# Warm-up products of a two-layer decoder: rounded, 512 columns wide, with a new order of issue

## The chip, the core and the metric

The kernel runs on one core of one Trainium2 chip. Its time is the device time of one execution in microseconds (us); of several runs the median counts. The core has five engines that work side by side: TensorE (in the profile PE for its products and PEld for the loads of stationary operands), VectorE (DVE), ScalarE (ACT), GpSimd (POOL) and SyncE (SP), which here issues most transfers. The transfers of the program and the blocks of the engines' own instructions are carried by the same 16 DMA engines.

## The reference

It computes a decoder trunk of two layers over a sequence of 256 tokens of width 1024, batch 1, in float32:

```
c_act = silu(c)
for layer in (0, 1):
    shift, scale, gate = split(c_act @ w_ada[layer] + b_ada[layer], 3)
    h = rms_norm(x, norm_g[layer]) * (1 + scale) + shift
    y = even_mixer(h) if layer == 0 else odd_mixer(h)
    x = x + gate * y
return rms_norm(x, final_g)
```

`even_mixer` projects h once, feeds a sliding-window attention with sinks and a three-branch sparse attention, multiplies each by a SiLU gate and projects the result out. `odd_mixer` does the same with a block-sparse attention, which at 256 tokens is plain causal attention within one block.

## The kernel before

The products with weights are kept accurate by splitting each operand into a rounded part and a remainder (`whi`, `wlo` of the weights, `hhi`, `hlo` of the activations). Three rounded products (type F32R) then stand for one in float32: hi by hi, hi by lo and lo by hi (`mm3`). A float32 product (type F32) that is no transpose goes through TensorE as two loads and two passes. A rounded product, and a transpose, is one load and one pass.

All operations are recorded first (`Plan.record`) and then issued in a fixed order, the list `ORDER` of their record numbers. `FLIP` lists operations that go to the other one of VectorE and ScalarE than the code names. Each engine runs its own instructions in the order of that list, so a later instruction waits behind an earlier one that is not ready.

The start of the program runs as follows. x and the small vectors are loaded. TensorE runs products of a tile of ones that nobody reads (12 into the bank of `ring_warm`, 20 into that of `keep`), so that it isn't idle ahead of its first real work. c is put through SiLU into `cz`; x is normalised and transposed into `bigA`. The columns of `w_ada` for shift and scale come in five groups (`START`). The first group covers 128 columns of shift and of scale: four transfers of 256 KB into `qT`. The second covers 256 columns of each: eight transfers of 256 KB, two each into a third `qT` tile, `gate`, `oT` and `kTb`. Of the second group, VectorE sums the rows that lie in `qT` and `gate` into `acc` (`start_sums`, d = 4), and TensorE sums those in `oT` and `kTb` directly and then adds `acc`, all in the bank `ps_m`. From a group's sums follow shift and scale (`shs`), from these `hhi` and `hlo`, and then the products of that piece of h with its rows of `w_in_even` (`start_mm`), which come through `raw` in two transfers a row (652 KB and 192 KB).

In the order before, the transfers of SP begin: x in two pieces, one of the first group, the 652 KB row piece, one of the first group, the 192 KB piece, two of the first group, then the second group as `oT`, `oT`, `qT`, `qT`, `gate`, `gate`, `kTb`, `kTb`, then the next rows of `w_in_even`. VectorE adds the `gate` rows to `acc` right after those of `qT`, then forms `hlo` of the first piece and, when TensorE has the sums of the second group, copies them out (`asb`). TensorE does 13 rounded products of the first piece ahead of the sums over `kTb` and `acc`.

Of the kernel before, what the change touches and what calls it, by code (L numbers as in the profile page):

```python
# [13 lines left out]
P = 128  # L14
# [21 lines left out]
49 7 6 4 0 1 9 21 22 23 2 3 47 5 91 41 42 48 92 89 24 25 26 27 28 29 30 93 73 88 50 31 90 32 74 99 58 33 75 34  # L36
98 35 51 77 59 94 52 76 36 46 44 45 60 54 37 53 10 11 38 61 12 13 14 63 95 78 79 15 97 16 132 17 126 96 64 128
101 127 18 19 20 62 129 100 102 103 104 105 106 107 108 109 110 111 112 113 114 115 116 117 130 133 55 83 158
118 65 56 66 68 80 67 119 159 84 85 121 86 120 81 131 69 122 174 175 176 177 178 179 180 181 168 82 70 143 160
140 170 134 123 137 87 171 39 161 40 124 149 138 169 172 155 150 146 144 71 162 135 173 72 147 141 125 163 182  # L40
183 184 185 186 187 188 189 190 191 192 193 152 194 142 195 153 201 165 196 136 197 151 199 198 164 154 156 202
148 203 157 139 200 238 207 226 204 205 239 240 166 214 227 208 228 206 220 209 167 232 215 235 212 236 241 268
221 280 242 243 269 218 223 281 233 210 145 229 230 278 216 213 237 222 244 211 250 270 234 282 259 262 271 251
283 224 252 279 225 247 219 265 284 256 272 231 245 257 285 263 273 286 287 288 289 290 291 292 293 217 294 295
296 297 264 298 258 299 307 274 246 300 248 301 249 275 303 302 260 266 253 308 254 309 255 267 261 324 304 336
311 305 310 337 333 277 345 318 325 306 346 339 313 276 338 312 342 319 314 343 372 326 316 344 315 348 373 380
322 8 381 320 378 379 375 374 377 376 472 530 334 327 328 382 335 360 366 361 383 362 329 349 340 341 350 347
369 330 384 331 332 354 385 363 351 357 317 386 387 388 389 390 391 392 393 394 395 396 397 321 355 398 356 323
399 367 405 400 368 401 364 402 358 359 406 365 370 407 371 352 403 442 409 443 408 430 436 411 473 418 410 353
433 424 527 420 445 404 431 434 412 446 413 425 421 533 427 428 416 432 439 422 474 414 423 475 1003 939 476 691  # L50
477 417 415 435 444 466 429 451 440 441 447 437 463 478 480 482 484 479 481 483 485 486 487 438 488 460 419 489
495 454 455 491 490 469 470 493 464 492 426 496 448 499 457 467 494 497 471 529 456 500 509 501 449 498 510 511
524 450 502 503 617 525 452 458 618 465 619 620 531 453 468 461 550 506 462 942 459 556 512 551 513 813 514 526
507 554 504 557 508 552 505 521 555 522 534 518 536 553 515 537 516 541 538 519 606 542 520 938 539 517 535 607
528 544 543 608 937 547 540 676 564 565 566 567 568 569 576 694 577 612 578 579 609 580 581 588 589 590 613 558
523 610 611 591 592 593 549 600 601 602 559 639 545 692 603 604 621 614 622 623 624 560 695 561 625 548 562 563
570 571 615 572 605 573 626 627 640 631 628 629 632 641 574 575 630 582 693 583 633 634 635 814 935 636 643 644
645 646 584 642 638 585 940 586 587 647 594 595 670 596 597 669 546 598 637 599 668 648 649 816 650 651 663 653
661 662 696 697 698 699 700 671 654 701 652 702 664 703 818 943 689 819 936 655 817 656 43 657 665 658 704 666
705 706 667 707 708 815 709 660 710 711 659 672 673 712 713 674 714 715 716 944 717 941 746 747 748 749 945 532  # L60
683 675 946 947 948 949 754 950 951 952 953 750 752 954 955 956 957 756 753 958 959 960 961 677 684 1029 751 678
774 775 776 777 962 1032 682 757 758 780 679 680 963 685 681 718 820 782 781 964 778 719 821 686 759 784 687 720
755 822 721 722 786 688 723 965 823 971 824 779 724 966 972 785 868 869 870 871 760 967 787 968 872 761 878 969
783 768 973 974 975 976 977 978 979 980 876 981 982 983 984 763 874 985 986 987 988 769 762 788 880 1150 879 789
970 896 897 898 899 1030 1218 989 877 764 765 881 904 990 796 825 906 725 991 873 902 726 826 791 727 728 992
729 900 730 875 731 993 732 827 616 908 766 797 994 882 998 995 1000 1001 999 1031 767 1087 1088 1089 1090 996
790 905 770 1002 771 1648 1221 997 1033 772 828 1091 829 1004 830 690 831 1005 832 883 733 1093 1006 773 734
1097 1007 901 833 1095 834 792 1092 1008 793 794 891 1113 1114 1115 1116 1151 885 795 1009 1010 1011 1012 903
1034 798 799 1013 800 835 735 909 736 836 884 837 838 801 839 1152 1037 737 738 890 739 740 907 1014 886 887
1015 888 1121 1096 840 1350 741 1016 742 1094 841 1349 1123 842 1038 843 1017 1039 889 1040 844 1117 845 1035  # L70
743 910 846 1119 847 848 849 911 1219 892 850 1122 1041 1042 1043 851 1118 1153 1154 1155 1156 919 1018 1036 744
893 852 1098 853 894 1044 1045 1019 1046 913 1339 1047 854 1220 855 912 856 1048 1049 895 1050 1051 1052 1020
1053 1054 857 1157 1222 858 1419 859 1159 914 915 916 1418 1163 802 803 804 805 806 807 808 809 1160 1021 1161
917 1022 1099 1223 918 1124 1179 1180 1181 1182 1120 1100 1023 745 1164 920 921 922 1055 1056 1102 1024 1057
1189 1058 1059 1107 1060 1025 1226 1227 923 1228 1125 1183 1061 1062 1126 1108 860 810 1063 1064 1229 1230 1026
1101 1027 1187 1162 861 1340 862 863 1127 1065 1231 864 1133 1232 1233 1234 1028 865 1235 1185 1224 1236 1237
1103 1341 1104 1105 924 925 926 927 928 929 930 931 1106 1158 1225 1426 1128 811 1276 1277 1278 1279 866 1351
1423 1109 1134 1422 1110 1111 1066 1165 1188 1238 1282 1239 1240 1241 1067 1112 1284 1068 1166 1286 1069 1174
1070 1242 1352 1243 1129 1130 1184 1131 1244 1285 1071 1245 1072 1073 1167 1074 1280 1075 1427 1246 1247 1248
1249 1250 1251 1252 1253 1254 1132 1420 1186 1190 1076 1077 812 1255 1173 1135 1136 1137 1168 1191 1421 1302  # L80
1303 1304 1305 1138 1436 1342 1343 1344 1345 1312 1428 1169 1287 1306 1170 1171 1429 1192 1256 867 1078 1172
1079 1257 1258 1080 1199 1308 1259 1260 1313 1261 1262 1263 1264 1265 1281 1266 1267 1268 1283 1269 1081 1082
1310 1437 1083 1194 1175 932 1176 1177 1084 1450 1311 1270 1346 1451 1178 1288 1452 1424 1646 1193 1271 1272
1273 1085 1453 1195 1196 1274 1197 1289 1086 1353 1354 1355 1356 1198 1200 1425 1359 1139 1140 1141 1142 1143
1144 1145 1146 1147 1148 1307 933 1309 1275 1432 1440 1433 1201 1361 1202 1203 1357 1454 1430 1204 1444 1445
1290 1446 1291 1447 1448 1363 1442 1449 1292 1149 1293 1294 1431 1205 1206 1207 1208 1209 1210 1211 1212 1213
1214 1379 1380 1381 1382 1438 1297 1314 934 1508 1296 1295 1315 1439 1317 1316 1298 1362 1299 1215 1300 1493
1455 1364 1441 1456 1492 1457 1216 1462 1347 1463 1301 1458 1385 1464 1358 1459 1217 1318 1322 1465 1319 1360
1434 1320 1460 1461 1323 1468 1469 1365 1321 1387 1470 1366 1443 1466 1367 1324 1325 1368 1326 1471 1467 1327
1474 1435 1374 1496 1472 1369 1370 1526 1497 1371 1328 1329 1330 1331 1332 1333 1334 1335 1336 1337 1389 1509  # L90
1372 1383 1527 1373 1390 1384 1375 1494 1376 1377 1386 1534 1535 1388 1558 1536 1378 1391 1475 1392 1537 1495
1393 1538 1559 1394 1560 1528 1473 1395 1400 1396 1510 1397 1399 1561 1338 1562 1511 1398 1476 1529 1348 1563
1401 1402 1403 1477 1404 1478 1498 1479 1405 1406 1407 1408 1409 1410 1411 1412 1413 1414 1499 1530 1415 1539
1649 1540 1531 1416 1650 1588 1417 1512 1513 1541 1542 1564 1565 1480 1481 1543 1486 1487 1482 1488 1483 1489
1484 1490 1485 1491 1544 1500 1532 1545 1778 1566 1546 1504 1547 1548 1533 1549 1567 1550 1655 1568 1551 1501
1552 1717 1553 1554 1505 1502 1555 1556 1656 1557 1506 1503 1514 1515 1516 1517 1582 1651 1507 1653 1583 1569
1839 1518 1584 1652 1570 1571 1572 1573 1574 1575 1576 1589 1659 1519 1590 1520 57 1521 1591 1522 1657 1577 1523
1578 1524 1592 1593 1525 1654 1594 1595 1596 1579 1598 1580 1660 1581 1597 1605 1606 1585 1599 1601 1600 1667
# [1302 lines left out]
```

## Time and profile before

| what | value |
|---|---|
| median of 3 runs | 294.72 us (294.68, 294.72 and 314.98) |
| the profiled execution | 295.43 us |
| its span, first to last instruction | 293.7 us |
| PE busy | 283.5 us |
| DVE busy | 253.0 us |
| ACT busy | 201.2 us |
| instruction blocks of the largest instruction queue | 17 packets, 0.28 MB |

The profiled execution took 1.73 us around its span, and is 0.71 us above the median of the runs. A busy PE in the profile can be a PE that runs at a slower pace, since ends of products are modelled. The idle time of an engine costs something only where another engine waits for its result.

### The profile page before, as it was taken

What the parts mean: (1) busy time and instruction counts of PE and PEld (TensorE: products, weight loads), DVE (VectorE), ACT (ScalarE), POOL (GpSimd) and SP (SyncE); (2) the same over time, 40 slices, a digit from 0 to 9 for tenths busy, and PEclk for the clock granted to TensorE, in tenths of its full rate; (3) what the DMA queues carried; (4) which work ended last, traced back from release to release, by engine and by line L of the source; (5) the groups of instructions that cost most, each with busy time, mean ns of one, the idle gap of its engine ahead of it and who ended that gap; (6) DMA issues with size and microseconds to landing.
All of it is one profiled execution on the core that took longest, in us unless ns stands there. A gap on an engine that the chain in (4) does not pass through costs nothing.

```text
span 293.7 us, 6077 instructions
## 1 busy us (share of the span) xinstructions
PE 283.5 (97%) x2244; PEld 243.5 (83%) x2244; DVE 253.0 (86%) x612; ACT 201.2 (69%) x513; POOL 5.5 (2%) x27
## 2 busy tenths in 40 slices
PE   8989999999999999999899999999999999999991
PEld 7868888997789888777667799999799899887891
DVE  0669999999999999999899868898699889889973
ACT  5554746695999999996398744466667377783821
POOL 2100000000000000000000000000000000000000
PEclk9999999999999999999999999999999999999998
DMA  7999999987996787799996449608927661604003
GB/s 260 364 385 377 383 355 353 311 287 237 342 400 212 264 281 293 213 323 361 305 372 216 146 143 329 243 4 296 351 71 249 237 234 34 227 27 145 1 15 129
DMA packets 50557, 71.76 MB, mean 244 GB/s; under 512 B 2792, under 2 KB 36192, under 8 KB 50528
## 3 DMA queue, kind: packets, MB, share of 16 engines
q1 hardware_dynamic: 50128, 70.95, 70.7%
q10 hardware_dynamic: 400, 0.43, 0.4%
q8 instruction: 17, 0.28, 0.4%
q14 instruction: 12, 0.10, 0.1%
HBM read 70.32 MB, written 1.06 MB: 243 GB/s over the span
## 4 chain that ended last, share of the span: by engine, by line
PE 73%; DVE 13%; DMA 8%; issue 2%; ACT 2%; SPq 0%; DVEq 0%
PE ps_pj L276 49%; PE ps_s L276 9%; PE ps_pt L276 6%; DVE raw L276 5%; PE ps_o L276 4%; PE ps_m L276 4%; DMA kTb<-in_w_ada_dram 3%; DMA raw<-in_w_ada_dram 2%; DVE wlo L276 2%; DMA qT<-in_w_ada_dram 2%; DMA xs<-in_x_dram 1%; DVE t L276 1%; DVE oT L276 1%; ACT t L276 1%; DVE bigA L276 1%
## 5 line engine op out<-in xcount | busy, mean ns | idle before, releaser
L276 ACT CAST whi<-raw 128x512 fp32r<-128x512 f32 (+2 forms) x108 | 71.6, 689 | 33.6 <-PE ps_pj L276 15.8
L276 DVE TENSOR_TENSOR wlo<-raw,whi 128x512 fp32r<-128x512 f32 (+2 forms) x92 | 70.8, 792 | 6.4 <-ACT whi L276 6.4
L276 PE MATMUL ps_pj<-hlo,whi 128*128 128x256 f32 x256 | 70.8, 284 | 0.0
L276 PE MATMUL ps_pj<-hhi,wlo 128*128 128x256 f32 x256 | 70.0, 284 | 0.3 <-DVE wlo L276 0.3
L276 PE MATMUL ps_pj<-hhi,whi 128*128 128x256 f32 x256 | 69.9, 284 | 0.0
L276 PEld LDWEIGHTS ps_pj<-hlo,whi 128*128 128x128 f32 x256 | 48.0, 189 | 0.6 <-issue 0.3
L276 PEld LDWEIGHTS ps_pj<-hhi,wlo 128*128 128x128 f32 x256 | 47.4, 189 | 0.7 <-DVE wlo L276 0.5
L276 PEld LDWEIGHTS ps_pj<-hhi,whi 128*128 128x128 f32 x256 | 47.4, 188 | 0.3
L276 ACT ACTIVATE sm<-sm,mn 128x256 f32<-128x256 f32 (+1 forms) x58 | 25.9, 449 | 6.9 <-DVE mn L276 6.9
L276 PE MATMUL ps_pj<-whi,hhi 128*128 128x512 f32 (+2 forms) x72 | 25.8, 368 | 0.5 <-ACT hhi L276 0.4
L276 PE MATMUL ps_pj<-whi,hlo 128*128 128x512 f32 (+2 forms) x72 | 26.1, 374 | 0.0
L276 PE MATMUL ps_pj<-wlo,hhi 128*128 128x512 f32 (+2 forms) x72 | 26.0, 370 | 0.0
L276 DVE SCALAR_TENSOR_TENSOR wlo<-raw,whi 128x512 fp32r<-128x512 f32 x32 | 20.6, 686 | 3.7 <-ACT whi L276 3.6
L276 PE MATMUL ps_pj<-wlo,ghi 128*128 128x512 f32 (+1 forms) x56 | 20.4, 368 | 0.0
L276 PE MATMUL ps_pj<-whi,ghi 128*128 128x512 f32 (+1 forms) x56 | 20.4, 369 | 0.0
L276 PE MATMUL ps_pj<-whi,glo 128*128 128x512 f32 (+1 forms) x56 | 20.0, 367 | 0.0
L276 ACT ACTIVATE sm<-sm,rc 128x256 f32<-128x256 f32 (+1 forms) x41 | 17.3, 449 | 2.3 <-DVE rc L276 2.3
L276 DVE SCALAR_TENSOR_TENSOR raw<-raw,cz,raw 128x1024 f32<-128x1024 f32 x14 | 17.9, 1276 | 1.0 <-DMA raw<-in_w_ada_dram 0.9
L276 DVE SCALAR_TENSOR_TENSOR acc<-raw,cz,acc 128x1024 f32<-128x1024 f32 x14 | 17.9, 1278 | 0.1
L276 PEld LDWEIGHTS ps_pj<-whi,hhi 128*128 128x128 f32 x72 | 13.6, 188 | 2.7 <-ACT hhi L276 1.2
L276 PEld LDWEIGHTS ps_pj<-whi,hlo 128*128 128x128 f32 x72 | 13.5, 188 | 2.5 <-DVE hlo L276 0.8
L276 PE MATMUL ps_pt<-ident,sm 128*128 128x128 f32 x87 | 15.5, 279 | 0.0
(252 smaller groups left out, 599.7 us busy)
## 6 DMA issues: line engine op xcount, KB each, us to landing
raw<-in_w_in_odd_dram SPq DMA_DIRECT2D x16, 1024.0 KB, 7.5
raw<-in_w_ada_dram SPq DMA_DIRECT2D x8, 1024.0 KB, 6.2
raw<-in_w_ada_dram SPq DMA_DIRECT2D x16, 512.0 KB, 5.2
raw<-in_w_in_even_dram SPq DMA_DIRECT2D x8, 652.0 KB, 7.2
raw<-in_w_in_even_dram SPq DMA_DIRECT2D x5, 1024.0 KB, 7.7
raw<-in_w_out_even_dram SPq DMA_DIRECT2D x4, 1024.0 KB, 5.4
raw<-in_w_out_odd_dram SPq DMA_DIRECT2D x4, 1024.0 KB, 5.0
qT<-in_w_ada_dram SPq DMA_DIRECT2D x12, 256.0 KB, 6.2
```

The costliest lines, as they stand in the source:

```text
L276: self.ops.append(dict(key=eng.key, deps=deps, fn=lambda: getattr(real, name)(*args, **kw)))
```

## The change

The tile of ones shrinks to two columns, which the table-loading activations still read. The products that nobody reads take a rounded tile of ones, 512 columns wide, that lies in the space of `ghi` (which is written for good only later in layer 0); `ghi` is therefore allocated earlier. A memset on VectorE fills those 512 columns ahead of the first product. The number of the products stays at 32. Each becomes one load and one pass of 512 columns in place of two loads and two passes of 128 columns.

`ORDER` and `FLIP` are replaced. Since one operation is added, every record number above 6 is one higher. Apart from that memset the operations are the same. At the start:

- SP: x in two pieces, one transfer of the first group, the 192 KB piece, one of the first group, the 652 KB piece, the two `qT` transfers of the second group, the last two of the first group, then `oT`, `oT`, `kTb`, `gate`, `kTb`, `gate`, then the next rows.
- ACT: c is fetched ahead of the two small matrices, and the first half of x is normalised ahead of the second.
- PE: 11 unread products, the transpose of c, 6 more, then transposes of x with the other 15 unread products in between; 12 rounded products of the first piece; the sums over `kTb` and `acc`; then the products with `hlo`.
- DVE: the two additions of `gate` rows to `acc` come after the shift and scale of the first group and the remainders `wlo` of its weights, then `hlo` of the first piece, then the copy of the sums (`asb`). Two copies of transposed x into `bigA` (128x512) move from ACT to DVE.
- Further on, `FLIP` moves 21 more operations from ACT to DVE and 19 from DVE to ACT (of those, five each way between the first projections and the end of layer 0's attention), and neighbouring instructions change places on all engines. The last 94 or so operations of PE keep their places.

```diff
-    ones = const([P, P], "ones")
+    ones = const([P, 2], "ones")
+    ghi = const([P, KT, S], "ghi", F32R)
+    ones_r = ghi[:, 0:2, :].rearrange("p a b -> p (a b)")
     ring_warm = bank("m")
+    V.memset(ones_r.bitcast(F32), 1.0)
     V.memset(ones, 1.0)
     dummy = const([P, 2], "dummy")
     A.activation(dummy[:, 0:1], ones[:, 0:1], AF.Exp)
     for _ in range(WARM):
-        T.matmul(ring_warm[:, :P], ones, ones, start=True, stop=True)
+        T.matmul(ring_warm, ones_r[:, :P], ones_r, start=True, stop=True)
     keep = bank("o")
     for _ in range(20):
-        T.matmul(keep[:, :P], ones, ones, start=True, stop=True)
+        T.matmul(keep, ones_r[:, :P], ones_r, start=True, stop=True)
...
-    ghi = const([P, KT, S], "ghi", F32R)
...
 ORDER = [int(i) for i in """
-49 7 6 4 0 1 9 21 22 23 2 3 47 5 91 41 42 48 92 89 24 25 26 27 28 29 30 93 73 88 50 31 90 32 74 99 58 33 75 34
...
+3 7 2 5 6 4 91 94 89 93 95 96 90 92 100 99 101 97 102 98 59 74 0 1 42 48 49 43 60 61 46 47 75 76 45 44 62 63 22
+23 24 25 26 27 28 29 30 31 32 51 133 52 53 54 78 129 77 131 33 34 35 36 37 38 69 70 71 72 55 64 79 80 65 10 11
...
```

## Rows read from the trace of the kernel before

**Rows 1.** Busy time of each engine by stretches of 20 us (us, instructions, clock, DMA).

```profile
core 0: us, PE busy (x) PEld busy (x) DVE busy (x) ACT busy (x) POOL busy (x), PEclk, DMA share, GB/s
0.00:20.00 20.00, 17.64 (x172) 15.56 (x173) 7.91 (x20) 10.15 (x19) 3.17 (x18) 1.00 0.95 333
20.00:40.00 20.00, 20.00 (x144) 16.94 (x143) 18.77 (x38) 10.79 (x23) 0.00 (x0) 1.00 1.07 381
40.00:60.00 20.00, 20.00 (x135) 17.60 (x130) 18.81 (x45) 14.39 (x39) 0.00 (x0) 1.00 1.00 323
60.00:80.00 20.00, 20.00 (x205) 16.72 (x204) 19.53 (x71) 15.89 (x52) 0.38 (x3) 1.00 0.90 297
...
120.00:140.00 20.00, 20.00 (x138) 14.88 (x137) 19.92 (x38) 17.44 (x44) 0.00 (x0) 1.00 0.94 329
140.00:160.00 20.00, 18.73 (x91) 13.05 (x90) 18.12 (x37) 13.95 (x33) 0.61 (x2) 1.00 0.90 304
160.00:180.00 20.00, 19.71 (x137) 18.03 (x138) 16.16 (x30) 12.05 (x24) 0.00 (x0) 1.00 0.55 174
```

**Rows 2.** The chain of waits in order of time, first 22 us (start us, us, what).

```profile
0.80 3.82 DMA xs<-in_x_dram
...
5.06 5.94 DMA qT<-in_w_ada_dram
...
11.01 7.55 DMA kTb<-in_w_ada_dram
...
18.61 0.86 PE ps_m L276 x24
19.47 0.67 PE ps_s L276 x2
...
20.25 0.23 PE ps_s L276
...
21.14 0.12 PE ps_pt L276
```

**Rows 3.** Who waited for whom, 17 to 20.2 us (us in total, times, longest).

```profile
ACT whi L276 <- DMA raw<-in_w_in_even_dram: 2.6, 1, 2.6
DVE asb L276 <- PE ps_m L276: 1.9, 1, 1.9
...
PE ps_m L276 <- DMA kTb<-in_w_ada_dram: 1.1, 1, 1.1
```

**Rows 4.** DMA traffic from 0 to 16.3 us, then queues from 16.3 to 18.6 us.

```profile
DMA packets 4988, 5.20 MB, mean 319 GB/s; under 512 B 294, under 2 KB 4583, under 8 KB 4988
...
q1 hardware_dynamic: 290, 0.88, 97.9%
q8 instruction: 1, 0.02, 3.2%
```

**Rows 5.** The page's row of that instruction queue over the whole span.

```profile
q8 instruction: 17, 0.28, 0.4%
```

**Rows 6.** Busy time and instructions from 0 to 16.3 and from 16.3 to 17.2 us.

```profile
0.00:16.30 16.30, 15.06 (x140) 13.89 (x141) 6.32 (x17) 9.56 (x18) 3.17 (x18) 1.00 0.94 319
16.30:17.20 0.90, 0.90 (x7) 0.66 (x5) 0.86 (x2) 0.38 (x1) 0.00 (x0) 1.00 1.06 413
```

**Rows 7.** Instructions in order of time, start of the span (start us, us, engine).

```profile
0.90 0.17 DVE L276 MEMSET ones<- 128x128 f32 x1 [0.90 <-PEq L1386]
...
1.71 3.84 PE L276 MATMUL ps_o<-ones 128*128 128x128 f32 x20
...
5.63 1.60 PE L276 MATMUL ps_o<-ones 128*128 128x128 f32 x12
...
14.20 0.37 PE L276 MATMUL ps_pt<-whi,hhi 128*128 128x256 f32 x1
...
14.45 0.48 DVE L276 TENSOR_SCALAR acc<-qT,cz 128x512 f32<-128x512 f32 x1
...
15.75 1.54 DVE L276 SCALAR_TENSOR_TENSOR acc<-gate,cz,acc 128x512 f32<-128x512 f32 x2
...
17.20 0.42 DVE L276 TENSOR_TENSOR hlo<-oT,hhi 128x256 fp32r<-128x256 f32 x1
```

**Rows 8.** DVE groups, shapes apart (busy us, mean ns).

```profile
L276 DVE COPY bigA<-ps_pj 128x512 f32<-128x512 f32 x4 | 2.7, 686 | 0.0
L276 DVE TENSOR_SCALAR sm<-sm,rc 128x128 f32<-128x128 f32 x9 | 2.4, 279 | 0.1
```

255 rows, old and new, of tables (FLIP, ORDER) are left out of this document.

## The prediction

> **What bounds the kernel now.** I read the busy time by stretches first [rows 1]. From 20 us on PE is full, and it has visible gaps only in 140 to 180 us (1.27 and 0.29 us). DVE is nearly as full: 57.11 of the 60 us from 20 to 80, and 19.92 of 20 in 120 to 140. So two engines share the bound from 20 to about 145 us, and PE alone holds it after 165. The reader should see that little is to be had there by moving instructions about. Only the first 20 us have room: 2.36 us on PE, 12 on DVE, 9.9 on ACT.
>
> The chain of waits says what those 20 us hang on [rows 2]: the loads of x, then of `qT`, then of `kTb`, which lands at 18.57 us. The list of waits [rows 3] shows three engines held at once: PE 1.1 us for `kTb`, DVE 1.9 us for PE's sums, ACT 2.6 us for the next rows of `w_in_even`, which travel behind `kTb`.
>
> Is that landing a matter of bandwidth? The transfers up to `kTb` sum to 1024 KB of x, 12 x 256 KB of `w_ada`, 652 + 192 KB of weights and 36 KB of small ones: 4976 KB, 5.10 MB. By 16.3 us 5.20 MB had moved [rows 4]. So the bytes were there about 2 us before the landing was told. What lies between is one packet of another queue, of instructions [rows 4]. There are 17 such packets of 16 KB, and they took 0.4% of 16 engines' 293.7 us [rows 5]: 18.8 us, or 1.1 us each. One packet occupies one of the 16 DMA engines, and a transfer that is spread over all of them has landed when the last has done its share. This is an inference: a `kTb` share queued behind the packet comes 1.1 us late.
>
> A block of 16 KB at 64 bytes holds 256 instructions. My count of the order gives 4488 loads and passes on PE, which makes 17.5 blocks and fits the 17 packets. So this is PE's own program, and it is asked for when PE has got to a certain instruction. At 16.3 us PE had started 281, at 17.2 us 293 [rows 6].
>
> **The change part by part.**
> *The unread products.* Before, 32 products are 64 loads and 64 passes; after, 32 and 32. PE's program is 64 instructions shorter, all ahead of the first projection. Time per product: 20 passes took 3.84 us and 12 took 1.60 [rows 7], so a product of two passes took 0.38, later 0.27 us. A rounded product of 512 columns steps at 0.23 us [rows 2]; early it may take up to twice that. Ahead of the second small transpose stand 17 products, 4.0 to 8.0 us. They start after a memset of 512 columns, between the 0.17 us of the 128-column one and the 0.48 us of a 512-column operation [rows 7]. I take 0.4. They end by 5.3 to 9.5 us. All this costs nothing as long as the first projection waits for loads, to 14.2 us [rows 7]; without that cover it would cost up to 2 us.
>
> *Where the block falls.* In the old order PE's count is 288 at the end of the 13 rounded products, just ahead of the `kTb` sums. In the new one the `kTb` sums begin at 224 and the `acc` sums end at 272. So 281 to 293 lies 5 to 10 products behind both. The packet then can't sit ahead of `kTb` or `gate`: those loads must have landed for PE to get there. Landing without the packet is between 16.3 (the bytes) and 17.5 us (18.57 less 1.1); I take 17.0. The next rows of weights move forward too, by up to 1.1 us of ACT's 2.6 us wait.
>
> The Trainium skill speaks against this step: "Runtime: NRT & Kernel Launch", section "Instruction fetch mechanics", has the engine fetch its next block of 256 instructions while it runs the current one, so that crossing a boundary costs little and is mostly hidden. By that the block would cost nothing, and the time would stay at 294.7. It is the first rival below.
>
> *The order of the loads.* The last two transfers of the first group now stand behind two of the second: 512 KB, about 1.4 us at the 0.38 MB per us of rows 1. The first projection moves from 14.2 to some 15.6 us. The 12 rounded products ahead of the `kTb` sums have as many columns as the 13 before (2.5 us at 0.23, 0.19 by proportion, and 0.12 for 512, 408 and 256 columns [rows 2]). They end at 18.1 us; with the sums PE is at 18.75. Before, PE waited in that time, so the delay is covered.
>
> *`gate` last.* Its rows go through DVE: 1.54 us for two additions [rows 7]. From 17.0 to 17.5 this gives 18.55 to 19.05. The four `acc` products follow, and `hlo`, which now stands behind the additions on DVE, takes 0.42 us [rows 7]: 19.0 to 19.5 us. PE needs it for its next product. Before, real products resumed at 19.47 [rows 2]. PE gains 0 to 0.5 us. Behind the additions also wait `asb` and the shift and scale of pieces 1 and 2.
>
> *DVE afterwards.* Its copy of the sums comes up to 0.5 us earlier, and with the weights there 1.1 us earlier it has `wlo` to do where it waited. So DVE gains 0.1 to 1.0 us. As DVE and PE share the bound up to 145 us, I take the middle, 0.6.
>
> *The flips and the rest.* Two copies of 0.69 us [rows 8] go to DVE inside its 12 idle us: nothing, while they lie there, and 1.4 us if they fell later. Up to the end of layer 0's attention five small operations go each way (0.28 us and up [rows 8]) and nearly cancel. What the neighbours' changes of place do after 20 us no row shows. Bounds: they can gain no more than a part of the 1.56 us of PE gaps in 140 to 180 and of the 2.89 us of DVE idle in 20 to 80 [rows 1], and may lose as much. I take zero, and 1.5 us either way for the range. The last 94 operations of PE keep their order, so the tail is the same. POOL's memsets and ACT's small loads are early and idle-covered: zero, up to 0.3 us.
>
> *Sum.* 295.43 (span 293.7 and 1.73 around it) - 0.6 = 294.8 for an execution like the profiled one, which stands 0.71 above the median of the runs. The median becomes 294.1.
>
> **The rivals.**
> *The packet was not the cause, or the gain is given back* (0.2): 294.7. For it: 16 other packets fall in the span, and PE shows no gap like that beside them; what DVE is given earlier may only wait later. Against: bytes there by 16.3, landing told at 18.57.
> *The new order also trims the gaps* (0.18): half of 1.56 and a quarter of 2.89 us, together 1.5 more: 292.6. For: these are the only stretches with room, and flips move operations there. Against: in 120 to 140 us PE and DVE are both full.
> *`gate` is caught* (0.13): slower. If the sequencer asks for the block well ahead of what PE has started, more than some 60 instructions ahead, the packet arrives before the last `gate` transfer. It then lands at 18.57 as `kTb` did, and 1.54 + 0.42 us of DVE still follow: 20.5 in place of 19.47, 1.0 to 1.1 us late on both engines: 295.8. The point that decides is whether the packet starts before `gate` has landed. Against: in the old trace the packet came with PE at 281 to 293 and waiting for `kTb` at 292, which leaves the sequencer little room to lead.
> *The wider products don't keep PE ready* (0.04): if PE stepped at half pace through the first piece, 12 products would take 5.0 in place of 2.5 us: 2.5 us more than the forecast and 0.6 of lost gain, 297.2. The granted clock reads 1.00 throughout rows 1, so nothing in the trace speaks for it.
>
> **How the numbers follow.** The forecast, 294.1, has 0.45, and its own width is 293.4 to 294.9. With rivals of 294.7, 292.6, 295.8 and 297.2 at the chances above, and 1.5 us either way for the order after 20 us, the range is 292.0 to 296.4. A change of 2%, 5.9 us, is about what a measurement of this kernel can tell from no change. It would need under 288.8 or over 300.6; no case gets there. I leave 0.02 for faster (gaps on three engines closing at once) and 0.03 for slower (half pace over more than one piece).
>
> **What would show it.** Right: 32 loads and 32 passes on ones; no wait of PE, DVE or ACT for a load of 1 us or more between 16 and 20 us; the first instruction packet after 18 us; sums over `kTb` and `acc` done and `hlo` products running by 19.0 to 19.5 us; the first `whi` of the second piece well ahead of 20.05. Then the lead of about 0.6 us should still be there at 100 us and where the last projection begins. Wrong: the packet still at 16 to 17 us, a landing of `gate` past 18, or a lead at 20 us that is gone by 145 us. The forecast fails most easily through the order of the middle, of which I know places but no waits.

## The result, and the profile after

The median rose from 294.72 to 298.71 us (297.69 to 299.17). The ratio to the kernel before is 1.0139, with a 95% interval of 1.0112 to 1.0165. So the change made the kernel slower by 1.4%, where the prediction had 0.2% faster, and the time lies above its range. It is still within the 2% that the chances called no change.

The profiled execution of after took 297.69 us (span 296.0), the shortest of its runs, while that of before, 295.43 us, was longer than four of the five runs of before in this comparison (the fifth, a slow one of 314.98 us, is left out of the ratio). So the two traces differ by 2.3 us and the medians by 4.0. Part of the loss can't be seen in this pair.

The kernel after, busy time by stretches, columns as in [rows 1]:

```profile
0.00:20.00 20.00, 18.41 (x138) 13.61 (x139) 9.31 (x23) 9.78 (x19) 3.07 (x18) 1.00 0.96 321
20.00:40.00 20.00, 19.47 (x119) 16.25 (x118) 18.27 (x38) 10.20 (x22) 0.00 (x0) 1.00 1.07 372
...
140.00:160.00 20.00, 17.48 (x82) 12.06 (x81) 16.82 (x32) 12.40 (x26) 0.63 (x3) 1.00 0.79 273
```

Against [rows 1] two things stand out. From 20 to 40 us PE, which was full, has a gap of 0.53 us, and the transfers move less (321 and 372 GB/s in place of 333 and 381). From 140 to 160 us, where layer 0 ends and the first weights of layer 1 come in, PE is idle for 2.52 us in place of 1.27.

The chain of waits of after at the start, which answers to [rows 2]:

```profile
1.79 4.83 DMA rows<-in_b_ada_dram
...
6.63 0.37 SPq L274
...
8.35 6.27 DMA oT<-in_w_ada_dram
...
14.63 8.44 DMA raw<-in_w_in_even_dram
```

`kTb` is no longer on it. But the small load of `b_ada`, which now is the last of the three on ACT's queue, holds SP until 6.63 us, and a row of `w_in_even` lands only at 23.07 us. That row is the third transfer of its kind; it stood at 22.15 us in before, and it now lies behind a transfer into `t`. PE waits for what comes of it:

```profile
24.80 0.45 PE L274 MATMUL ps_o<-wlo,hhi 128*128 128x408 f32 x1 [0.53 <-DVE wlo L274]
```

The instruction block moved as forecast. The queues of after from 18.8 to 20.2 us, which answer to [rows 4]:

```profile
q1 hardware_dynamic: 327, 0.54, 105.5%
q8 instruction: 1, 0.02, 5.1%
```

Then the layer change. PE's waits in after from 138 to 170 us (us in total, times, longest); before had one of 0.8, one of 0.4 and one of 0.3 there:

```profile
PE ps_pj L274 <- ACT t L274: 1.4, 1, 1.4
PE ps_pj L274 <- ACT hhi L274: 1.1, 1, 1.1
PE ps_pj L274 <- DVE hlo L274: 0.4, 1, 0.4
```

The 0.8 us of before is this line:

```profile
PE ps_s L276 <- DVE wlo L276: 0.8, 1, 0.8
```

It is about what that execution has above its median, and the profiles of late_sqrt, products_alone, products_padded and before_shifted, all with the old order, don't have it.

And what ACT of after did ahead of the first of after's three waits, in order of time:

```profile
146.79 1.14 ACT L274 CAST whi<-raw 128x512 fp32r<-128x512 f32 x2 [1.86 <-DMA raw<-in_w_in_odd_dram]
...
149.07 1.13 ACT L274 CAST whi<-raw 128x512 fp32r<-128x512 f32 x2
150.11 0.58 ACT L274 COPY t<-ps_m 128x512 f32<-128x512 f32 x1
150.70 1.28 ACT L274 ACT_TABLE_LOAD   x1
152.00 0.20 ACT L274 ACTIVATE parts<-parts 128x1 f32<-128x1 f32 x1
...
152.61 1.33 ACT L274 ACTIVATE t<-xs,parts 128x512 f32<-128x512 f32 x2
```

The reader should see an engine without a pause for 7 us, a table load for the square root in its middle, and both halves of the normalised tokens on it, one behind the other. In the order before, a dummy Sqrt brought this load at 139.4 us, while ACT was idle. In the new order that dummy stands behind the real Sqrt (places 1841 and 1581).

### The profile page after: what moved, and what is told of

Read it like the earlier page. It is cut to its first block, busy times and chain, and to the rows that moved or that the text cites. A ratio compares the mean times of both kernels' runs of the same rounds, so it can differ in the third digit from the quotient of the medians.

```text
span 296.0 us, 6012 instructions
## 1 busy us (share of the span) xinstructions
PE 284.9 (96%) x2212; PEld 241.4 (82%) x2212; DVE 253.1 (86%) x617; ACT 201.1 (68%) x509; POOL 5.8 (2%) x27
## 4 chain that ended last, share of the span: by engine, by line
PE 76%; DVE 10%; DMA 7%; ACT 3%; issue 2%; SPq 1%; ACTq 0%; DVEq 0%
PE ps_pj L274 51%; PE ps_s L274 10%; PE ps_pt L274 6%; PE ps_o L274 6%; PE ps_m L274 3%; DMA raw<-in_w_in_even_dram 3%; DMA oT<-in_w_ada_dram 2%; ACT t L274 2%; DMA rows<-in_b_ada_dram 2%; DVE raw L274 2%; DVE t L274 2%; DVE wlo L274 1%; DVE oT L274 1%; DVE bigA L274 1%; DVE sm L274 1%
## 5 line engine op out<-in xcount | busy, mean ns | idle before, releaser
L274 PE MATMUL ps_pj<-hhi,whi 128*128 128x256 f32 x256 | 70.7, 286 | 0.0
L274 ACT ACTIVATE sm<-sm,mn 128x128 f32<-128x128 f32 (+1 forms) x58 | 26.1, 452 | 7.1 <-DVE mn L274 7.1
L274 PE MATMUL ps_pj<-wlo,ghi 128*128 128x512 f32 (+1 forms) x56 | 20.2, 367 | 0.0
L274 DVE TENSOR_TENSOR t<-ps_pj,tb 128x512 f32<-128x512 f32 (+2 forms) x22 | 12.0, 586 | 7.4 <-PE ps_pj L274 7.4
L274 ACT ACTIVATE whi<-raw 128x512 fp32r<-128x512 f32 x16 | 9.7, 626 | 10.4 <-PE ps_pj L274 9.3
L274 ACT ACTIVATE sm<-sm,rc 128x256 f32<-128x256 f32 (+1 forms) x36 | 15.7, 461 | 1.6 <-DVE rc L274 1.5
```

The source lines that it names most:

```text
L274: self.ops.append(dict(key=eng.key, deps=deps, fn=lambda: getattr(real, name)(*args, **kw)))
```

## The experiments

My first theory, T1: the time is lost in the layer change, by that table load and by the order of the two halves of the tokens. Its rivals, R1: it is lost in the prologue and in the loads; R2: it is a spread from run to run. All medians and ratios stand in one table; each ratio is to runs of before in the same series. A is the start of the last product of layer 0's attention in the profiled execution, B the way from there to the last product of the kernel, us:

| kernel | median | ratio to before, 95% | A | B |
|---|---|---|---|---|
| before | | 1 | 137.9 | 149.2 |
| after | 298.71 | 1.0139 (1.0112 to 1.0165) | 138.4 | 151.3 |
| sqrt_ahead | 298.03 | 1.0135 (1.0106 to 1.0164) | 140.1 | 151.5 |
| late_sqrt | 295.59 | 1.0039 (1.0024 to 1.0054) | 137.8 | 148.7 |
| sqrt_behind_ghi | 298.40 | 1.0138 (1.0121 to 1.0155) | 139.0 | 151.8 |
| products_alone | 295.41 | 1.0037 (1.0022 to 1.0051) | 138.6 | 148.0 |
| order_alone | 298.39 | 1.0142 (1.0120 to 1.0164) | 138.8 | 151.5 |
| products_padded | 294.38 | 1.0004 (0.9991 to 1.0017) | 137.8 | 148.2 |
| before_shifted | 295.36 | 1.0038 (1.0025 to 1.0050) | 139.1 | 148.4 |
| after_padded | 298.25 | 1.0129 (1.0108 to 1.0150) | 138.8 | 153.5 |
| new_to_140 | 297.34 | 1.0082 (1.0054 to 1.0111) | 138.9 | 150.7 |
| old_to_140 | 297.40 | 1.0106 (1.0081 to 1.0131) | 138.2 | 151.0 |
| new_to_60 | 297.66 | 1.0121 (1.0101 to 1.0141) | 140.2 | 148.6 |
| old_new | 296.06 | 1.0057 (1.0038 to 1.0077) | 137.4 | 149.4 |
| new_old | 296.38 | 1.0071 (1.0046 to 1.0096) | 138.7 | 149.0 |
| halves_back | 300.10 | 1.0192 (1.0173 to 1.0210) | 138.7 | 153.3 |
| old_new_order | 299.48 | 1.0172 (1.0149 to 1.0196) | 137.5 | 154.6 |
| old_flips | 294.66 | 1.0017 (1.0001 to 1.0034) | 137.4 | 148.5 |
| new_old_loads | 302.48 | 1.0282 (1.0262 to 1.0302) | 141.2 | 153.0 |
| after_loads | 304.93 | 1.0350 (1.0323 to 1.0377) | 141.9 | 155.0 |

**The table load.** Three kernels move the dummy Sqrt and nothing else.

```diff
 sqrt_ahead, ORDER of after (1589 is the dummy Sqrt, 1590 the real one, 1417 the cast of oT to ghi)
-1651 1416 9 1417 1532 1418
+1651 1416 9 1589 1417 1532 1418
 late_sqrt, ORDER of before (1588 the dummy, 1589 the real one)
-1531 1416 1650 1588 1417 ... 1575 1576 1589 1659
+1531 1416 1650 1417 ... 1575 1576 1589 1588 1659
 sqrt_behind_ghi, ORDER of after
-1416 9 1417 1532 1418
+1416 9 1417 1589 1532 1418
```

sqrt_ahead: 

> The changed kernel with one operation of its order moved: the dummy Sqrt that loads ScalarE's table in the layer change goes from behind the real Sqrt to right behind the dummy Exp, about 139 us, where ScalarE has idle time. T1 (the loss is in the layer change, and the 1.28 us table load at 150.7 us is on its chain): 0.7 to 1.5 us faster than the changed kernel, so about 297.4 us and a ratio of 1.009; the table load is seen near 139 us and not after the sum of squares. R1 (the loss comes from the prologue and the loads): no change, 298.7. R2 (the change only spreads from run to run): no change.

late_sqrt: 

> The kernel before with one operation moved, the other way round: the dummy Sqrt goes from right behind the cast of oT to ghi (139.4 us) to right behind the real Sqrt, as in the changed order. T1 (a table load on the chain of the layer change costs its 1.28 us): 295.3 to 296.0 us, the load at about 150.5 us directly ahead of the real Sqrt. R1 and R2: 294.6, because TensorE has other products to run in that time.

sqrt_behind_ghi: 

> The changed kernel with the dummy Sqrt moved to right behind ScalarE's cast of oT to ghi, the place that it has in the kernel before; the run before put it one operation too early, ahead of that cast, where TensorE waited 1.5 us for ghi. T1: 1.0 to 1.5 us less than the changed kernel, 297.0 to 297.7 us, and no wait of TensorE for ghi or for the first t of the layer change over 1 us. R1 and R2: 298 to 298.7 us as before.

In the order before, the late load costs 0.39%, 1.2 us (0.7 to 1.6 by the interval), about its whole length:

```profile
148.72 1.28 ACT L277 ACT_TABLE_LOAD   x1
150.02 0.20 ACT L277 ACTIVATE parts<-parts 128x1 f32<-128x1 f32 x1
```

The Trainium skill ("ScalarE: Activation LUTs", section "What ACT_TABLE_LOAD costs") gives 1.28 us and another 1.38 for a drain. The trace agrees with the first; no run here shows the second: ScalarE goes on 0.02 us behind the load. In the new order moving the load gives nothing back. PE's waits in sqrt_behind_ghi, 138 to 168 us, show why:

```profile
PE ps_pj L276 <- ACT ghi L276: 1.3, 1, 1.3
PE ps_pj L276 <- ACT hhi L276: 1.3, 2, 1.1
PE ps_pj L276 <- DVE hlo L276: 0.4, 1, 0.4
```

The wait of 1.4 us for `t` is gone and one of 1.3 us for `ghi` stands in its place, because the cast ahead of that on ACT waited for rows of `w_out_even` until 140.9 us (137.9 in after). All three kernels with the dummy early in the new order have that cast so late (140.9, 140.7 and 140.5 us); in sqrt_ahead the wait is put down to a transfer of `w_ada`. Why is open. T1 in its first form had fallen.

**The products and the addresses.**

```diff
 products_alone: ORDER and FLIP of before, the rounded products of after
 order_alone: ORDER and FLIP of after
-        T.matmul(keep, ones_r[:, :P], ones_r, start=True, stop=True)
+        T.matmul(keep[:, :P], ones_r[:, :P].bitcast(F32), ones_r[:, :P].bitcast(F32), start=True, stop=True)
 products_padded: products_alone with; after_padded: after with
-    ones = const([P, 2], "ones")
+    ones = const([P, P], "ones")[:, 0:2]
 before_shifted: before with
     ones = const([P, P], "ones")
+    const([P, 8], "gap")
```

products_alone: 

> The kernel before, its order and its choice of engines, with the unread products alone made rounded ones of 512 columns (and the wide memset ahead of them). R1 (products and the shifted instruction block cost the time): 296 to 298.7 us. T1: 294.1 to 294.9 us, since the layer change is that of before; the table load stays near 139 us. By the prediction's own forecast the block comes behind kTb and the time is 294.1.

order_alone: 

> The changed kernel, its order and its choice of engines, with the unread products back to unrounded ones of 128 columns (two passes each, so 64 more instructions on TensorE ahead of the projections). T1: about 298.7 us like the changed kernel, with the table load at about 150.7 us on the chain. R1 in the form that the products cost the time: back to 294.7 to 295.5 us. If the order was made for the new products and the old ones push the instruction block ahead of kTb again: up to 1 us more, 299.7.

The order alone makes all of the loss, and yet the products alone cost 0.37%. Their trace gave the reason: their transfers move fewer bytes in the same busy share. The 1024-byte packets between 10 and 20 us took 46 ns in before (median of 2117) and 51 in products_alone (of 2048). The one thing that both have in common with after is the narrow tile of ones. It takes 32 bytes of a partition in place of 512, so the tiles behind it start 480 bytes earlier: the first of `raw` at 123168 in place of 123648. Three kernels test that.

products_padded: 

> The rounded products in the order of before, as in the products alone, with the constant of ones given its old 512 bytes per partition again (2 columns of it are used), so that every tile behind it starts where it started before modulo 512 bytes; the narrow constant had moved the weight tiles from a multiple of 256 bytes to 32 bytes past one. R1 in a new form, the layout (the 1024-byte packets of the weights take 51 in place of 46 ns between 10 and 60 us because of their addresses): packets back at 46 ns, 1.0 us less than the products alone, 294.0 to 294.6 us. If the products themselves cost the time: 295.4 us, packets at 49 to 51 ns.

before_shifted: 

> The kernel before with nothing but an unused constant of 32 bytes per partition behind the ones, which moves the weight tiles to 32 bytes past a multiple of 256. Layout: packets of 1024 bytes at 49 to 51 ns, and 295.0 to 295.6 us. If the products made the packets slow: 46 ns and 294.5 us.

after_padded: 

> The changed kernel with the constant of ones at its old 512 bytes, nothing else. Layout: packets of 1024 bytes at 46 ns and 0.7 to 1.2 us less than the changed kernel, 297.2 to 297.8 us; the rest of its loss (order) stays. If addresses don't matter, or the layer change doesn't wait for loads: 298.4 us.

With the addresses back, the products cost nothing in the end (1.0004, packets 46 ns); with the addresses moved and nothing else, the kernel before loses 0.38%, 1.1 us (packets 51 ns). The stretches 0 to 20 and 20 to 40 us, first of products_padded:

```profile
0.00:20.00 20.00, 18.48 (x141) 13.84 (x142) 8.23 (x21) 10.78 (x20) 3.18 (x18) 1.00 0.93 335
20.00:40.00 20.00, 20.00 (x144) 16.89 (x143) 18.90 (x38) 10.11 (x22) 0.00 (x0) 1.00 1.07 383
```

then of before_shifted:

```profile
0.00:20.00 20.00, 18.34 (x176) 16.01 (x177) 8.56 (x23) 10.15 (x19) 3.18 (x18) 1.00 0.96 318
20.00:40.00 20.00, 19.14 (x131) 15.94 (x134) 17.96 (x35) 10.51 (x23) 0.00 (x0) 1.00 1.07 372
```

The last columns are the lesson: as high a busy share, 3 to 5% fewer bytes, and PE with a gap from 20 to 40 us. That the move costs time is shown; why is not. The Trainium skill ("DMA: Bandwidth & Descriptors", section "How a descriptor splits into AXI transactions") says of reads that each transaction must start at a multiple of 256 bytes, so that a descriptor that doesn't start at one pays for bytes that it doesn't use. What moved here is where the transfers write. The runs don't bear this out as the cause. The slow packets fill `oT`, `qT`, `gate` and `kTb`, which start 96, 0, 32 and 96 bytes past a multiple of 256 in before and 128, 32, 64 and 128 past one in before_shifted: only `qT` left such a multiple, and all four slowed down. The packets into `raw`, which moved from 0 to 32 as well, are larger and took 200 ns at either place. The shift was tried with one size, in one direction.

The products are not free at the start. In products_padded the first projection comes at 15.22 us in place of 14.20 [rows 7]:

```profile
15.22 0.36 PE L277 MATMUL ps_pt<-whi,hhi 128*128 128x256 f32 x1
```

Against late_sqrt, which has the old products at the same addresses, that microsecond is gone by 127 us, and nothing of it is left in the median.

In the changed kernel the padding brings little (1.0129; the intervals overlap, so a gain of up to some 1 us isn't excluded), short of the 297.2 to 297.8 us that were expected. Column A says why: the new order reaches the layer change at 138.7 to 138.8 us with the addresses right (new_old, after_padded) and at 138.4 to 139.0 with them moved (after, order_alone, sqrt_behind_ghi, new_to_140, halves_back; sqrt_ahead, at 140.1, stands apart). In the old order it is 137.4 to 137.9 against 138.2 to 139.1. So by these single profiles the new order loses that microsecond already, in another way, and it is not lost twice.

**Where in the order.** Five kernels take the first operations of one order and the rest, as it stands, from the other, with the choice of engines that goes with each.

```diff
 new_to_140:  first 1516 of after, rest of before     new_to_60: first 571 of after, rest of before
 old_to_140:  first 1524 of before, rest of after
 new_old:     new_to_140 with the padded ones         old_new:   old_to_140 with the padded ones
```

new_to_140: 

> The rounded products and the new order with its choice of engines for the first 1516 operations (to about 140 us), and then what is left in the order of before, with the choice of engines of before, the layer change among it. T1: 2 to 3.5 us faster than the changed kernel, 295.2 to 296.7 us. R1 (lost before 140 us): 298 to 298.7 us, as nothing before 140 us is undone.

old_to_140: 

> The rounded products, the order of before with its choice of engines for 1524 operations (to about 140 us, with the dummy Sqrt at its early place), then the rest in the new order with its choice of engines. T1 without its table load (the order of the two token halves in the layer change): 296.4 to 297 us, 1 to 1.5 us over the 295.4 of the products alone. R1 (all is lost before 140 us): 295.4 us.

new_to_60: 

> The rounded products, the new order with its choice of engines for the first 571 operations (to about 60 us), then the rest in the order of before, its choice of engines with it. R1 (lost in the prologue and its loads): 296.8 to 297.5 us, as with the new order to 140 us. T1: 295.0 to 295.7 us, at most the cost of the products themselves.

old_new: 

> Rounded products with the padded ones (so the addresses of before), the order and engines of before to about 140 us, the new ones from there. The dummy Sqrt lies early. If the new order behind 140 us costs by itself, whatever came before it: 295.8 to 296.6 us, 1.5 to 2.2 over the padded products (294.4), and waits of TensorE of 2.5 to 3 us between 138 and 168 us. If it cost only because loads were late there: 294.4 to 295.0 us, since now they are not.

new_old: 

> Padded products, the new order and engines to about 140 us, those of before from there, the dummy Sqrt early. If the new order ahead of 140 us costs about 1.1 to 1.3 us by itself, as the runs with shifted addresses say: 295.5 to 295.9 us. If that loss was the slower packets: 294.4 to 294.8 us.

With right addresses: products_padded 0.04%, the new order ahead of 140 us 0.67% more (new_old), behind it 0.53% more (old_new); the sum, 1.24%, is what after_padded has, 1.29%. With moved addresses the parts are 0.45% ahead and 0.69% behind. Each is uncertain by 0.2 to 0.3%. So the new order costs 1.3 to 2.0 us ahead of 140 us and 1.6 to 2.0 us behind it, also with the packets at 46 ns. new_to_140 (297.34) lies between what R1 and T1 expected of it: part of the loss stands on either side. The median of new_to_60 tells little on the prologue: its profile loses another microsecond between 60 and 70 us, where its two orders are joined (A is 140.2).

The part ahead of 140 us is lost in the prologue and right behind it. Counted by the columns of the products that PE has begun (the unread ones aside), new_old is behind products_padded by 0.2 us at 20 us, 1.5 at 26 and 1.8 at 137. The same count has after behind by 0.6, 1.4 and 1.5 us. PE's waits in new_old from 20 to 30 us; products_padded has none there:

```profile
PE ps_pj L277 <- ACT hhi L277: 0.5, 1, 0.5
PE ps_o L277 <- DVE wlo L277: 0.4, 1, 0.4
```

The part behind 140 us shows in PE's waits of old_new from 138 to 170 us, where the dummy Sqrt is early and no load holds an engine for more than 0.4 us:

```profile
PE ps_pj L276 <- ACT hhi L276: 1.3, 2, 1.1
PE ps_pj L276 <- DVE hlo L276: 0.4, 1, 0.4
```

The wait of 1.1 us stands in seven of the eight profiles with the new order and engines there (after_padded lacks it), and in none with the old. The chain of waits of after leads up to the 1.1: VectorE's sums of the second half of the tokens are in front of the last pieces of the first half, for which ACT waits.

```profile
155.88 0.61 DVE t L274
...
156.51 0.69 DVE xs L274
...
157.47 0.75 DVE t L274
...
158.58 0.81 ACT t L274 x2
...
159.42 0.41 ACT hhi L274
159.83 0.04 issue
159.87 0.50 PE ps_pj L274
```

**What in the order.**

```diff
 halves_back: sqrt_behind_ghi, and records 1583 to 1645 without 1589 in their order of before
 among themselves, each on its engine of before (operations that need another moved up are moved back)
 old_new_order: old_new with FLIP of before
 old_flips: products_padded with FLIP of after for the records of the layer change
 new_old_loads, after_loads: new_old and after_padded with all loads (ahead of 140 us; to the end)
 in their order of before, as far as the work allows
```

halves_back: 

> The changed kernel with the dummy Sqrt behind the cast to ghi, and the 62 operations of the two token halves in the layer change (residual sum, norm, transposes, shift and scale, rounding) in their order of before among themselves, each on its engine of before. T1 as it now stands (the second half's sums and the first half's last pieces queue behind each other on VectorE, and ScalarE waits 1.5 us): 1.2 to 2.2 us less than with the dummy alone, 296.2 to 297.2 us, and the idle time of TensorE between 140 and 180 us down from about 3.0 to about 1.2 us. If the layer change only shows what was lost before it: 298.4 us.

old_new_order: 

> The same as the kernel before it in this list with one difference: each operation is on its engine of before, so only the order behind 140 us is new. If the choice of engines costs (both halves of the first normalized tokens on ScalarE, one behind the other): 0.5 to 1 us less than with the new engines. If the order costs (the second half's sums on VectorE ahead of the first half's last pieces): the same time, or more, as the order was made for the other engines.

old_flips: 

> The padded products in the order of before, with the new choice of engines for the operations of the layer change only (6 of its small operations and 2 behind them change engines). If the choice of engines costs by itself: 295.0 to 295.6 us, 0.6 to 1.2 over the padded products. If only the order costs: 294.2 to 294.7 us.

new_old_loads: 

> The kernel with the new order to about 140 us and the old one behind it (padded products, 296.4 us), with the loads ahead of 140 us issued in their order of before, on ScalarE's queue too (b_ada first); two loads stay swapped and a few operations of VectorE move behind a load that they need. If the order of the loads makes the loss ahead of 140 us (waits of 0.5 to 0.9 us at 20 to 26 us for rows that come late): 294.9 to 295.7 us, no wait of TensorE over 0.3 us between 20 and 30 us. If the order of the other work makes it: 296.4 us or more, as that order was made for the other loads.

after_loads: 

> The changed kernel with padded ones (298.3 us) and all loads to the end in their order of before, as far as the work allows; TensorE's own order is untouched. If late loads make most of the loss, ahead of and behind 140 us: 295.5 to 297 us, and the DMA engines don't fall idle at 152 to 156 us. If the loss behind 140 us is the order on ScalarE and VectorE: 297 to 298 us, better by the prologue alone.

The choice of engines in the layer change alone (8 operations) costs little (0.13% over products_padded). The four kernels that put back only the order, the loads or the engines of a part are slower than both whole orders, by 1.7 to 3.5% against before; the five that join whole parts lie between the two. halves_back (300.10 us) and after_loads (304.93) lie outside all that was expected of them. In new_old_loads the waits at 20 to 30 us are gone, as expected, but the first projection starts at 17.97 us in place of 15.42, and more is lost later. So these runs don't price the loads or the halves by themselves: order, loads and engines were made for each other, and putting back one of them is a third order. Within the two parts of the order, what costs how much stays open, and the reading of the chain above is not shown to be the cause.

**The clock.** In the profiled execution of after_padded PE waited 1.0 and 1.8 us, up to 152.6 and up to 155.2 us, and the granted clock fell during the second wait (columns as in [rows 1]):

```profile
152.00:154.00 2.00, 0.89 (x5) 0.58 (x5) 1.36 (x3) 1.97 (x5) 0.00 (x0) 1.00 0.08 23
154.00:156.00 2.00, 0.76 (x4) 0.76 (x5) 1.67 (x6) 1.80 (x4) 0.00 (x0) 0.60 0.00 0
156.00:158.00 2.00, 2.00 (x7) 1.51 (x6) 1.24 (x3) 1.13 (x3) 0.00 (x0) 0.50 0.65 141
...
160.00:162.00 2.00, 2.00 (x8) 1.58 (x7) 0.85 (x3) 1.08 (x3) 0.00 (x0) 0.69 1.08 368
162.00:164.00 2.00, 2.00 (x10) 1.64 (x9) 1.81 (x5) 2.00 (x7) 0.00 (x0) 1.00 1.09 387
```

0.50 is the lower of the two levels, 1.2 GHz. Two products of it, and one after it:

```profile
159.99 0.63 PE L276 MATMUL ps_pj<-whi,hhi 128*128 128x512 f32 x1
160.42 0.63 PE L276 MATMUL ps_pj<-wlo,hhi 128*128 128x512 f32 x1
...
161.96 0.39 PE L276 MATMUL ps_pj<-whi,hhi 128*128 128x512 f32 x1
```

A product steps at 0.43 us in place of 0.23, which over the ten of that width in the stretch makes 2.0 us. That execution took 300.24 us, the longest of its five, at a mean granted clock of 0.987; the other four have 0.994 to 0.998. In after the waits of the profiled execution were 1.4 and 1.1 us, further apart, and the clock stayed at 1.00. In new_old_loads and after_loads it falls too, at 146 to 150 us, behind waits of 0.9 and 1.2, and of 0.7 and 1.4 us; their mean clock is 0.987 to 0.990 in two of four and four of six executions.

For after this doesn't support R2, and the loss is clear of the spread (1.0112 to 1.0165). Its five executions have a mean clock of 0.994 to 0.997, so none shows such a stretch, and 299.17 us, the longest, was run at 0.997. The spread of after, and the 1 us by which its median exceeds the profiled execution, stay open.

## Why the prediction was wrong

- **The packet and `kTb`: the mechanism right, the price wrong.** The block did come behind the landings of `kTb` and `gate`, at 18.9 us, and the wait for `kTb` is gone. But late_sqrt, whose order is that of before up to 139 us, has its block at 16.54 us, 0.2 us later than before, and doesn't wait for `kTb` at all:

```profile
17.07 0.40 PE L277 MATMUL ps_s<-wlo,hhi 128*128 128x512 f32 x1
17.40 0.65 PE L277 MATMUL ps_m<-kTb,cz 128*32 128x128 f32 x16
17.86 0.40 PE L277 MATMUL ps_m<-acc,cz 128*32 128x128 f32 x8
18.19 0.50 PE L277 MATMUL ps_s<-whi,hhi 128*128 128x512 f32 x1
```

  The inference that a share of `kTb` came late behind the packet is borne out by the landings of the 16 shares of each transfer in the traces. In before 15 shares of the last `kTb` transfer had landed by 17.03 us and the 16th at 18.57; in late_sqrt all had landed by 17.00, as the prediction took it. From the block on, one share of every transfer lands 0.8 to 1.7 us behind the others in 18 of the 20 traces; the other two don't tell. So the stall comes or doesn't come by some tenths of a microsecond, and of the two profiles with this start of the program one has it.

  What failed is the term "DVE gains 0.1 to 1.0 us", of which the sum took 0.6. late_sqrt, without the stall, is 1.21 us ahead of before at the `kTb` sums (17.40 against 18.61 us [rows 2]). Further on it loses the lead, and at the same product ahead of the layer change 0.11 us of it is left, first before, then late_sqrt:

```profile
139.63 0.40 PE L276 MATMUL ps_pj<-whi,ghi 128*128 128x512 f32 x1
139.52 0.40 PE L277 MATMUL ps_pj<-whi,ghi 128*128 128x512 f32 x1
```

  products_padded has the shorter program in the order of before, its block at 18.05 us, `kTb` landed by 16.95 and a ratio of 1.0004. So the 0.6 measures nothing, clear of noise. The first rival (0.2, 294.7) was right in its second form, the gain is given back. The 0.71 us by which the profiled before stands above the median isn't the stall either: about as much went to its wait of 0.8 us in the layer change. The rule in "Runtime: NRT & Kernel Launch", section "Instruction fetch mechanics", of the Trainium skill has a block's boundary mostly hidden. For the time of the kernel the runs agree with it (1.0004).
- **The tile of ones: left out.** The prediction priced the products and the memset, not the 480 bytes by which the narrower tile moves all those behind it. A shift of that kind costs 1.1 us in the old order (before_shifted); in the new one its price isn't told from nothing.
- **The order of the loads: right within 0.3 us to 20 us, wrong behind it.** The first projection came at 15.91 us (forecast 15.6), the sums over `kTb` at 18.58, `hlo` products at 19.64 (19.0 to 19.5). `gate` landed at 17.60 us (17.0 to 17.5), and DVE waited 1.9 us for it. The first `whi` of the second piece moved forward, from 20.05 to 19.21 us. But the third row transfer landed later than before, and PE waited 0.53 us for it at 24.80. "ACT's small loads are early and idle-covered" failed at `b_ada`, which held SP until 6.63 us; no run prices that.
- **"I take zero, and 1.5 us either way", for the order after 20 us: the step that made the miss.** Parts of the order measure 1.3 to 2.0 us ahead of 140 us, most of it between 20 and 26 us, and 1.6 to 2.0 us behind, all losses; together they are most of the loss. What within the two parts costs how much stays open. The cap was worked out from the gaps that the old trace had. Gaps cap a gain, but a new order can open new ones, and a loss has no such cap. The moved dummy Sqrt could have been read in `ORDER` itself; its price in the old order, 1.2 us, would have shown which side is the likelier one, though moving it alone brings nothing back in the new order.
- **The other rivals.** The gaps were not trimmed. The wider products kept PE ready, with a clock of 1.00 to 40 us. `gate` was not caught by the block in after, but in order_alone, which has the order of after and its block at 16.55 us, it was. There 15 shares of the last `gate` transfer had landed by 17.60 us and the 16th at 18.80. DVE waits for it and PE for DVE, from 14 to 26 us first in order_alone, then in after:

```profile
DVE acc L276 <- DMA gate<-in_w_ada_dram: 3.3, 1, 3.3
PE ps_m L276 <- DVE acc L276: 1.4, 1, 1.4
...
DVE acc L274 <- DMA gate<-in_w_ada_dram: 1.9, 1, 1.9
```

  The medians don't show it (1.0142 and 1.0139): order_alone is 1.2 us behind after at 20 us, and 0.2 at 26.4. So most of this delay is made up again, as the lead of late_sqrt is lost.

## What to carry to other kernels

When an order is replaced, list what moved across an engine's idle time first: table loads, small loads, memsets. Bound a gain by the gaps that exist, but a loss by the work that has lost its cover. A tile that shrinks moves all tiles behind it, so look at the start of the buffers that transfers fill. And before a stall is made the ground of a forecast, see whether a second execution has it, and whether anything behind it would keep the time that it gives back.

## What the runs showed of the hardware

- All tiles behind the ones moved by 32 bytes (before_shifted): 51 in place of 46 ns for a 1024-byte packet (10 to 20 us), 318 GB/s in the first 20 us in place of 335 (products_padded, unmoved), 1.1 us of the kernel. Which addresses are slow, and why, isn't shown.
- A 16 KB block of instructions is one packet on one of the 16 DMA engines, and from it on one share of each transfer lands 0.8 to 1.7 us behind the other 15 (18 of 20 traces). Whether an engine waits for that depends on some tenths of a microsecond, and no median here shows it.
- Two waits of TensorE, of 1.0 and 1.8 us, ended within 3 us of each other; 1.2 GHz was granted during the second and for some 7 us in all, in one profiled execution. Waits of 1.4 and 1.1 us that lay 6 us apart left the clock at 1.00 in another.
- A table load on ScalarE's busy path took 1.28 us and cost 1.2 us of the kernel (0.7 to 1.6) in the old order; in the new one moving it gave nothing back.
